# Gates' products by Strassen's algorithm beside the attention, the branches' projections behind it

## The chip, the cores and the metric

The kernel runs on one core of one Trainium2 chip. The metric is the device time of one execution, in microseconds (us), median of three runs; the kernel before takes 1975.72 us (1972.22 to 1982.68). A core has a matrix engine (TensorE, PE in the profile, which also shows its weight loads as PEld), a vector engine (VectorE, DVE), an engine for activations and copies (ScalarE, ACT), a general engine (GpSimd, POOL), and queues from which DMAs are issued; this kernel issues nearly all of them from SyncE (SP). SBUF is the memory on the chip, PSUM the banks that matmuls accumulate into.

## The reference

One layer over 1024 tokens of width 1024, all in float32. The part that the change touches:

```python
z_a, z_bx, z_by, z_q, z_k, z_v, z_g = split_cols(h @ w_in[l], IN_SIZES)      # h = rms_norm(x)
y_a = rwkv7_mixer(z_a, ...) @ proj_a[l]                     # 512 x 1024
y_b = rglru_mixer(z_bx, z_by, ...) @ proj_b[l]              # 512 x 1024
y_c = dilated_attention_mixer(z_q, z_k, z_v, ...) @ proj_c[l]   # 256 x 1024
gates = jax.nn.sigmoid(z_g.reshape(bsz, seq, N_BRANCHES, D_MODEL))
merged = gates[:, :, 0] * y_a + gates[:, :, 1] * y_b + gates[:, :, 2] * y_c
x = x + merged @ w_out[l]
...
x = x + jnp.square(jax.nn.relu(u)) @ mlp_down[l]            # u = rms_norm(x) @ mlp_up[l]
```

`z_g` has 3 x 1024 columns. The attention has three groups of four heads, with dilations 1, 4 and 16; their outputs are weighted by their softmax denominators and summed to the 256 rows of y_c.

## The kernel before, in words

Activations lie transposed, channels on the 128 partitions and tokens along a row. A matmul takes 128 channels x 128 columns of weights against 128 x 512 tokens (a half), into one PSUM bank. To hold float32 accuracy each operand is split in a high part and a low part (`hi` is a cast by ScalarE, `lo` the difference, by GpSimd or VectorE), and `mm3` issues three matmuls for one product: high by high (L233), high by low (L234), low by high (L235). `load_w` reads weights into `wraw`, a ring of two buffers, and splits them into `whi` and `wlo`, rings of three.

The stages follow each other: norm and RG-LRU, then RWKV with the projections of Q, K and V between its steps, then from 799.4 to 1259.9 us the attention with the gates and the branches' projections, then `w_out` and the MLP.

In that third stage the attention runs in six units, two chunks `cc` of 128 channels times three groups `g`. A unit loads its Q and K (`load`: two tiles `z0`, `z1`), scales K and loads the bias (`prep`), and then goes through four steps `sp`: logits `l` on TensorE (L1014), the bias and the maximum on VectorE (`lg`, `nm`), the exponential on ScalarE (L1033), transposes `pt` (L1044), a copy by ScalarE, and the products with V, `o` (L1059). `combine_rows` transposes a unit's maxima and sums (`stt`, L1068) and sends them through DRAM (`st_d`, then `row`). `combine(cc)` makes the weights of the groups of one chunk, sends them through DRAM (`cw_d`), spreads them over the partitions (`cb`), and sums the groups' outputs to a half of `yc`.

Between these steps `filler` hands out pieces of the generator `fill`, so that TensorE has wide products while the other engines work. They come from `gate_ab` (the products `zg` and projections `pj` of the branches b and a) and `gate_c_z` (`zg` of branch c); `gates_c` does branch c's projection behind the attention. A `zg` piece is a half of a column tile, 24 matmuls, followed by a tanh; a `pj` piece has 12 matmuls for a half, and VectorE multiplies it with (1 + tanh). The partial sums of the branches go through DRAM as `mg_d`. The split branches, `yh` and `yl`, are made from `yb_d`, `ya_d` and `yc_d`, the raw rows (`yr`) passing through `wraw`.

Each engine works through its instructions in order. A scheduler with a simulated timeline sets that order when the kernel is built; within it, `tc.issue_after(pins[-lag].ins)` keeps a filler from being issued before the logits of a tile some steps back. SP hands out its DMAs in order too: one that must wait holds those behind it.

Of the kernel before, what the change touches and what calls it, by code (L numbers as in the profile page):

```python
# [18 lines left out]
P = 128  # L19
# [105 lines left out]
def hybrid_block(ctx, tc, io, out, dbg=None):  # L125
# [15 lines left out]
    yc_d = dr.tile([P, T], F32, name="yc_d")  # L141
# [99 lines left out]
    def gemm_pieces(w2d, c0, n, hh, hl, nm, evac, w=None, halves=(0, 1)):  # L241

        hi, lo = w or load_cols(w2d, c0, n, nm)
        for hf in halves:
            ps = pg.tile([P, 512], F32, tag="g", name=f"g_{nm}_{hf}")
            mm3(ps[:n, :], [(hi[:, k, :], lo[:, k, :], hh[hf][:, k, :], hl[hf][:, k, :]) for k in range(KT)])
            evac(ps, hf)
            yield
# [10 lines left out]
    def norm_split(xns, gkey, hh, hl, ks, nm):  # L259

        for k in ks:
            ps = psum("w", 2, f"nt_{nm}{k}")
            for i in range(4):
                PE.transpose(ps[:, i * P : (i + 1) * P], xns[i][:, k * P : (k + 1) * P], ident)
            gcol = pc(gkey, k)
            last = A.activation(hh[:, k, :], ps, AF.Copy, scale=gcol)
            V.scalar_tensor_tensor(hl[:, k, :], ps, gcol, hh[:, k, :], ALU.mult, ALU.subtract)
        return last

    w_in = io["w_in"][0]  # L270
# [55 lines left out]
    ths, yc, pws = {}, [], []  # L326

    def load_pc(m):

        raw = wp.tile([P, 2, 256], F32, tag="wraw", name=f"p2r{m}", bufs=2)  # L330
        S.dma_start(raw, io["proj_c"][0][:, m * P : (m + 2) * P].rearrange("(k p) c -> p k c", p=P))
        wh = gt.tile([P, 2, 256], F32R, tag="pwh", name=f"p2h{m}", bufs=1)
        wl = gt.tile([P, 2, 256], F32R, tag="pwl", name=f"p2l{m}", bufs=1)
        A.copy(wh, raw)
        G.tensor_tensor(wl, raw, wh, ALU.subtract)
        return wh, wl

    gt_p = tc.tile_pool(name="gt", bufs=1)
    gt = gt_p.__enter__()
    gy = gt  # L340
    gy_p = tc.tile_pool(name="gy", bufs=1)
    gy2 = gy_p.__enter__()
    zs = gate_c_z(tc, pieces, gt, ths)

    def fills():
        yield from gate_ab(tc, io, pieces, pg, gt, gy2, wp, ya_d, yb_d, load_w, mm3)
        for cc in range(2):
            yc.append([gt.tile([P, T], F32R, tag=t, name=f"{t}2{cc}", bufs=2) for t in ("yh", "yl")])
        raw = wp.tile([P, T], F32, tag="wraw", name="yr2", bufs=2)
        S.dma_start(raw, yc_d)  # L350
        A.copy(yc[0][0], raw)
        V.tensor_tensor(yc[0][1], raw, yc[0][0], ALU.subtract)
        pws.append(load_pc(0))
        for _ in range(4):
            next(zs)
            yield

    fill = fills() if "mixers_only" not in dbg else iter(())
    if "no_attn" not in dbg:
        attention(tc, io, dbg, psum, der, cg, yc_d, yc, bias_d, sst, rk_d, cw_d, v_d, qk_d, fill)  # L360
    for _ in fill:
        pass
    gy_p.__exit__(None, None, None)
    if "mixers_only" in dbg:
        gt_p.__exit__(None, None, None)
        hpool.__exit__(None, None, None)
        return
# [14 lines left out]
def attn_values(tc, io, hh, hl, load_w, mm3, pg, wp, v_d):  # L382
# [4 lines left out]
    for g in range(3):  # L387
        wv = [load_w(w_in[512 * q : 512 * q + 512, C_VV + 256 * g : C_VV + 256 * g + 256].rearrange("(k p) c -> p k c", p=P),
                     [P, 4, 256], f"wv{g}{q}") for q in range(2)]
        for s in range(8):  # L390
            ts_ = slice(s * P, (s + 1) * P)
            ps = pg.tile([P, 512], F32, tag="g", name=f"v{g}{s}")
            mm3(ps[:, 0:256], [(hh[:, k, ts_], hl[:, k, ts_], wv[k // 4][0][:, k % 4, :], wv[k // 4][1][:, k % 4, :]) for k in range(KT)])
# [578 lines left out]
def attention(tc, io, dbg, psum, der, cg, yc_d, yc, bias_d, sst, rk_d, cw_d, v_d, qk_d, fill):  # L972
# [4 lines left out]
    with tc.tile_pool(name="ac", bufs=1) as ac, tc.tile_pool(name="au", bufs=2) as au:  # L977
        zt, rqks, vts, biases, stats, ogs, pins = {}, {}, {}, {}, {}, {}, []

        def load(cc, g):  # L980
            for x in range(2):
                z = zt[(cc, g, x)] = au.tile([P, T], F32, tag=f"z{x}", name=f"z{x}_{g}{cc}", bufs=2)
                S.dma_start(z, qk_d[g, x, cc])

        def prep(cc, g):

            u = f"{g}{cc}"
            bias = biases[(cc, g)] = au.tile([P, 2, 256], F32, tag="bias", name=f"bias{u}", bufs=2)
# [90 lines left out]
        def combine(cc):  # L1079
# [24 lines left out]
            for hf in range(2):  # L1104
# [12 lines left out]
                if cc == 0:  # L1117
                    S.dma_start(yc_d[:, sl], y)
                elif yc:
                    A.copy(yc[1][0][:, sl], y)  # L1120
                    V.tensor_tensor(yc[1][1][:, sl], y, yc[1][0][:, sl], ALU.subtract)
# [17 lines left out]
        load(*units[1])  # L1139
        for n, (cc, g) in enumerate(units):  # L1140
# [23 lines left out]
        filler(7, 1)  # L1164
# [25 lines left out]
def gate_ab(tc, io, pieces, pg, gt, gy2, wp, ya_d, yb_d, load_w, mm3):  # L1190
# [3 lines left out]
    steps = [(b, m) for b in (1, 0) for m in range(KT)]  # L1194
    ys, wts, ths = {}, {}, {}

    def z_steps(b, m):

        def ev(ps, hf):
            th = ths[(b, m, hf)] = gt.tile([P, H], F32, tag="th", name=f"th{b}{m}{hf}", bufs=4)  # L1200
            A.activation(th, ps, AF.Tanh, scale=0.5)

        yield from pieces(C_Z + b * D + m * P, P, f"zg{b}{m}", ev)

    def load_y(b):
        for k in range(4):
            raw = wp.tile([P, T], F32, tag="wraw", name=f"yr{b}{k}", bufs=2)
            S.dma_start(raw, (yb_d if b else ya_d)[k * P : (k + 1) * P, :])
            pool = gt if k < 2 else gy2
            h = pool.tile([P, T], F32R, tag="yh", name=f"yh{b}{k}", bufs=2)  # L1210
            l = pool.tile([P, T], F32R, tag="yl", name=f"yl{b}{k}", bufs=2)
            A.copy(h, raw)
            (G if k % 2 else V).tensor_tensor(l, raw, h, ALU.subtract)
            ys[(b, k)] = (h, l)

    def proj_steps(b, m):
        if m % 2 == 0:
            w = io["proj_b" if b else "proj_a"][0][:, m * P : (m + 2) * P]
            wts[b] = load_w(w.rearrange("(k p) c -> p k c", p=P), [P, 4, 256], f"p{b}{m}")
        if m == 0:  # L1220
            load_y(b)
        wh, wl = wts[b]
        ms = slice((m % 2) * P, (m % 2 + 1) * P)
        for hf in range(2):
            sl = slice(hf * H, hf * H + H)
            th = ths.pop((b, m, hf))
            if b == 0:
                tb = gt.tile([P, H], F32, tag="tb", name=f"tb{m}{hf}", bufs=2)
                S.dma_start(tb, io["mg_d"][0][m, :, sl])
            ps = pg.tile([P, 512], F32, tag="g", name=f"pj{b}{m}{hf}")  # L1230
            mm3(ps, [(wh[:, k, ms], wl[:, k, ms], ys[(b, k)][0][:, sl], ys[(b, k)][1][:, sl]) for k in range(4)])
            V.scalar_tensor_tensor(th, th, 1.0, ps, ALU.add, ALU.mult)  # L1232
            if b == 0:
                G.tensor_tensor(th, th, tb, ALU.add)
            S.dma_start(io["mg_d"][1 - b][m, :, sl], th)
            yield

    yield from z_steps(*steps[0])
    for i, s in enumerate(steps):
        if i + 1 < len(steps):  # L1240
            yield from z_steps(*steps[i + 1])
        yield from proj_steps(*s)


def gate_c_z(tc, pieces, gt, ths):

    for m in range(KT):

        def ev(ps, hf):
            th = ths[(m, hf)] = gt.tile([P, H], F32, tag="th", name=f"th2{m}{hf}", bufs=4)  # L1250
            tc.nc.scalar.activation(th, ps, AF.Tanh, scale=0.5)

        yield from pieces(C_Z + 2 * D + m * P, P, f"zg2{m}", ev)


def gates_c(tc, io, psum, gt, zs, ths, mhi, mlo, yc, load_pc, pw, mm3):
# [3 lines left out]
    for m in range(KT):  # L1260
        if m % 2 == 0:
# [392 lines left out]
```

## Time and profile before

| | us |
|---|---|
| median of three runs | 1975.72 (1972.22 to 1982.68) |
| profiled execution | 1980.51 |
| its span | 1978.7 |
| norm and RG-LRU, RWKV | 0 to 799 |
| attention, gates, projections | 799.4 to 1259.9 |
| w_out | 1259.9 to 1354 |
| MLP up, MLP down | 1354 to 1650, 1650 to 1979 |

The profile is of one execution. A line of a group gives the line of the kernel, the engine, the operation, the tile written and the tiles read, shape and count, then the busy time in us and the mean of one in ns, then the idle time ahead of it and what ended that. A row by stage gives the stretch, its length, and for PE, PEld, DVE, ACT and POOL the busy time with the number of instructions, then the granted clock of TensorE, the DMA share and GB/s. A row of the waits gives who waited for whom, the total in us, how often, and the longest. A row of the timeline gives start, duration, engine, line and operation, with the idle time ahead in brackets. An SP row's duration is that of handing out; when the data is there is seen from who waits for it.

### The profile page before, as it was taken

The numbers are of one execution on the slowest core, as the hardware profiler recorded it, in microseconds if no ns is written. First come the engines' busy times: TensorE is split into PE (matmuls) and PEld (weight loads), VectorE is DVE, ScalarE is ACT, GpSimd is POOL, SyncE is SP. The second block draws the span as 40 slices with busy tenths as digits, with TensorE's granted clock in tenths as the row PEclk, the third lists the DMA queues.
The fourth block names the chain that finished last, engine by engine and source line by source line (L and its number), as shares of the span: only waits on it lengthen the run. The fifth ranks groups of instructions, "written<-read, shape, count | busy, mean of one in ns | idle before, by whom it ended". The sixth has DMA issues, their size and how long they took to land. (4 is left out here: it accounts for less than half of the span.)

```text
span 1978.7 us, 29639 instructions
## 1 busy us (share of the span) xinstructions
PE 1918.6 (97%) x11754; PEld 1528.5 (77%) x11754; DVE 1143.5 (58%) x1868; ACT 717.3 (36%) x1184; POOL 727.8 (37%) x590
## 2 busy tenths in 40 slices
PE   8999999999999999899999999999999999999999
PEld 6776677787677878777777778887888888888887
DVE  5546356657656564323333344436877567988875
ACT  5675223243333331333334322245323323333332
POOL 1333434442452340211263242244343343444543
PEclk9999999999999998999999999999999999999999
DMA  4122312222221221633354333552433439544231
GB/s 147 54 61 79 91 52 62 55 60 52 54 70 40 66 65 38 197 121 102 100 170 128 102 116 99 185 183 107 158 140 149 163 136 381 195 146 181 96 123 69
DMA packets 187056, 227.08 MB, mean 115 GB/s; under 512 B 38072, under 2 KB 132949, under 8 KB 186918
## 3 DMA queue, kind: packets, MB, share of 16 engines
q1 hardware_dynamic: 186742, 225.18, 34.7%
q8 instruction: 92, 1.51, 0.3%
q14 instruction: 46, 0.38, 0.1%
q0 software_dynamic: 160, 0.02, 0.0%
q10 hardware_dynamic: 16, 0.00, 0.0%
HBM read 163.42 MB, written 64.10 MB: 115 GB/s over the span
## 5 line engine op out<-in xcount | busy, mean ns | idle before, releaser
L233 PE MATMUL g_zg<-hh,wh_zg 128*128 128x512 f32 x384 | 155.3, 404 | 0.0
L234 PE MATMUL g_zg<-hl,wh_zg 128*128 128x512 f32 x384 | 152.5, 397 | 0.0
L235 PE MATMUL g_zg<-hh,wl_zg 128*128 128x512 f32 x384 | 152.3, 397 | 0.0
L1374 POOL TENSOR_TENSOR wl_d<-dr,wh_d 128x1024 fp32r<-128x1024 f32 x40 | 101.0, 2525 | 127.5 <-ACT wh_d L1373 116.2
L1374 DVE TENSOR_TENSOR du<-dq,du 128x1024 fp32r<-128x1024 f32 x56 | 124.0, 2215 | 23.5 <-ACT du L1373 22.8
L226 POOL TENSOR_TENSOR wl_zg<-wr_zg,wh_zg 128x1024 fp32r<-128x1024 f32 x24 | 57.5, 2395 | 164.1 <-ACT wh_zg L225 143.2
L233 PE MATMUL dx<-wh_d,du 128*128 128x512 f32 x256 | 99.7, 389 | 0.5 <-DVE acc L1554 0.5
L234 PE MATMUL dx<-wl_d,du 128*128 128x512 f32 x256 | 99.6, 389 | 0.0
L235 PE MATMUL dx<-wh_d,du 128*128 128x512 f32 x256 | 99.5, 389 | 0.0
L1373 ACT CAST wh_d<-dr 128x1024 fp32r<-128x1024 f32 x40 | 42.1, 1052 | 142.1 <-PE dx L235 72.8
L233 PEld LDWEIGHTS g_zg<-hh,wh_zg 128*128 128x128 f32 x384 | 73.0, 190 | 18.0 <-issue 3.6
L235 PEld LDWEIGHTS g_zg<-hh,wl_zg 128*128 128x128 f32 x384 | 72.8, 190 | 16.5 <-issue 1.5
L234 PEld LDWEIGHTS g_zg<-hl,wh_zg 128*128 128x128 f32 x384 | 72.9, 190 | 15.7 <-issue 1.8
L234 PE MATMUL g_z<-hl,wh_z 128*128 128x512 f32 x192 | 77.1, 402 | 0.0
L235 PE MATMUL g_z<-hh,wl_z 128*128 128x512 f32 x192 | 77.0, 401 | 0.0
L233 PE MATMUL g_z<-hh,wh_z 128*128 128x512 f32 x192 | 76.5, 399 | 0.4 <-DVE zsq L428 0.4
L773 DVE TENSOR_SCALAR s<-ac,wc 64x64 f32<-64x64 f32 x128 | 36.0, 281 | 69.2 <-PE ac L769 66.8
L1374 POOL TENSOR_TENSOR wl_a<-ur,wh_a 128x1024 fp32r<-128x1024 f32 x15 | 46.8, 3117 | 72.9 <-ACT wh_a L1373 72.9
L1374 POOL TENSOR_TENSOR wl_s<-ur,wh_s 128x1024 fp32r<-128x1024 f32 x16 | 42.5, 2658 | 79.2 <-ACT wh_s L1373 79.2
L1232 DVE SCALAR_TENSOR_TENSOR th<-th,pj 128x512 f32<-128x512 f32 x32 | 21.8, 684 | 73.7 <-PE pj L235 71.3
L226 POOL TENSOR_TENSOR wl_wo<-wr_wo,wh_wo 128x1024 fp32r<-128x1024 f32 x16 | 38.4, 2403 | 68.4 <-ACT wh_wo L225 68.4
L1033 ACT ACTIVATE lg<-lg,nm 128x128 f32<-128x128 f32 (+1 forms) x96 | 42.2, 441 | 56.6 <-DVE nm L1031 56.6
(664 smaller groups left out, 5706.4 us busy)
## 6 DMA issues: line engine op xcount, KB each, us to landing
dq<-u_d SPq DMA_DIRECT2D x56, 512.0 KB
ur<-in_mlp_up_dram SPq DMA_DIRECT2D x16, 1024.0 KB
dr<-in_mlp_down_dram SPq DMA_DIRECT2D x16, 1024.0 KB
wr_zg<-in_w_in_dram SPq DMA_DIRECT2D x24, 512.0 KB
mg_d<-th SPq DMA_DIRECT2D x32, 256.0 KB
tb<-mg_d SPq DMA_DIRECT2D x32, 256.0 KB
wr_wo<-in_w_out_dram SPq DMA_DIRECT2D x16, 512.0 KB
wr_z<-in_w_in_dram SPq DMA_DIRECT2D x12, 512.0 KB
```

The source lines that it names most:

```text
L226: E.tensor_tensor(lo, raw, hi, ALU.subtract)
L233: PE.matmul(ps, lh, rh, start=first and i == 0, stop=False, skip_group_check=skip)
L234: PE.matmul(ps, lh, rl, start=False, stop=False, skip_group_check=skip)
L235: end = PE.matmul(ps, ll, rh, start=False, stop=last and i == n - 1, skip_group_check=skip)
L773: V.tensor_scalar(ns[half[h], :], pb[h][half[h], 128 * j + 64 * c : 128 * j + 64 * c + 64], wc[half[h], 2 * i + c : 2 * i + c + 1], None, ...
L1033: A.activation(lg[:, q, los[q] : 256], lg[:, q, los[q] : 256], AF.Exp, bias=nm[:, q : q + 1], accum_out=stat[:, 1, h, 2 * sp + q : 2 * sp ...
L1232: V.scalar_tensor_tensor(th, th, 1.0, ps, ALU.add, ALU.mult)
L1373: A.copy(hi, src)
L1374: split.last = E.tensor_tensor(lo, src, hi, ALU.subtract)
```

## The change

The products of the gates change from `gate_ab`/`gate_c_z` to `gate_z`. It takes column tiles in twelve pairs. The first two pairs are done as before (`n_plain`). For the other ten, the 2x2 blocks are two column tiles by two halves of k (weights) and two halves of k by two halves of the tokens (activations), and Winograd's form of Strassen's algorithm makes four blocks of result from seven block products. The activations' combinations T1 to T4 are made once, T1, T2 and T4 by VectorE, T3 by GpSimd, with high and low parts; the weights' combinations are made for each pair, three adds and a low part by VectorE, the other low parts by GpSimd. Three of the products are copied from PSUM by ScalarE (`held`) and added by VectorE.

All tanh results go to DRAM (`th_d`) and come back in the new stage `gates`, behind the attention, where all three branches' projections are made and summed. The branch rows y_b are loaded to a pool `yp` opened behind the attention's pools, y_c and y_a through `wraw`. `combine` writes both chunks to `yc_d`.

In the attention, the buffers of Q and K and of the bias are one and not two; the next unit is loaded and prepared after a unit's last step, with three fillers behind. The fillers' counts change to the smaller pieces (12 matmuls each), and the filler(7) ahead of `combine(1)` goes.

```diff
-    hpool = tc.tile_pool(name="hT", bufs=1)
+    hpool = tc.tile_pool(name="hT", bufs=1, side="right")
...
+    fill = gate_z(tc, w_in, ht, h2, hp, gt, wp, pg, th_d, load_cols, mm3, late)
+    attention(tc, io, dbg, psum, der, cg, yc_d, bias_d, sst, rk_d, cw_d, v_d, qk_d, fill)
+    yp_p = tc.tile_pool(name="yp", bufs=1)
+    yp = yp_p.__enter__()
+    ys = {}
+
+    def load_y(pool, src, b, n, raw):
+
+        for k in range(n):
+            r = raw(k)
+            S.dma_start(r, src[k * P : (k + 1) * P, :])
+            h, l = (pool.tile([P, T], F32R, tag=f"y{b}{k}{x}", name=f"y{x}{b}{k}") for x in "hl")
+            A.copy(h, r)
+            (G if k % 2 else V).tensor_tensor(l, r, h, ALU.subtract)
+            ys[(b, k)] = h, l
+
+    yraw = lambda b: lambda k: wp.tile([P, T], F32, tag="wraw", name=f"yr{b}{k}", bufs=2)
+    load_y(yp, yb_d, 1, 4, lambda k: yp.tile([P, T], F32, tag=f"y2{k // 2}{'hl'[k % 2]}", name=f"yr1{k}"))
+    late.append(lambda: load_y(yp, yc_d, 2, 2, yraw(2)))
     for _ in fill:
         pass
...
+    load_y(ya, ya_d, 0, 4, yraw(0))
+    last = gates(tc, io, psum, pg, gt, ya, wp, th_d, ys, mhi, mlo, load_w, mm3)
...
-                z = zt[(cc, g, x)] = au.tile([P, T], F32, tag=f"z{x}", name=f"z{x}_{g}{cc}", bufs=2)
+                z = zt[(cc, g, x)] = au.tile([P, T], F32, tag=f"z{x}", name=f"z{x}_{g}{cc}", bufs=1)
...
-                    filler(1.2)
+                    filler(0.4 if i else 2)
                 V.tensor_copy(ogs[(cc, g)][:, sp * 256 : (sp + 1) * 256], po[:, 0:256])
-                if sp == 0 and n > 0 and n + 1 < 6:
+                if sp == 3 and n + 1 < 6:
                     load(*units[n + 1])
-                if sp == 1 and n + 1 < 6:
                     prep(*units[n + 1])
+                    filler(3)
                 if sp == 2 and n == 3:
                     combine(0)
             combine_rows(cc, g)
-        filler(7, 1)
         combine(1)
...
+        for c in two:
+            total(V, F["T1"][:, c], c, [b("B12", 0, c), b("B11", 0, c), (b("B12", 1, c), add), (b("B11", 1, c), sub)])
+            total(V, F["T2"][:, c], c, [b("B22", 0, c), F["T1"][:, c], (b("B22", 1, c), add)])
+            split(V, "T2", c, F["T2"][:, c])
+            split(V, "T1", c, F["T1"][:, c])
...
+        for j, (nm, bk, first) in enumerate((("B11", X, True), ("B21", Y, True), ("T2", X, False), ("T1", Y, True),
+                                            ("T3", X, False), ("B22", Y, False), ("T4", X, False))):
...
+            wh, wl = ops.pop((n, j))
+            mm3(bk, [(wh[:, k, :], wl[:, k, :], B[nm][0][:, k, :], B[nm][1][:, k, :]) for k in range(4)], first=first, skip=True)
+            if j in (0, 2, 3):
+                t = tile(f"{n}{j}")
+                A.copy(t, bk)
+                held[j] = t
+            elif j < 6:
+                t = held[{1: 0, 4: 3, 5: 2}[j]]
+                V.tensor_tensor(t, bk, t, ALU.add)
+                done(b, *{1: (m0, 0), 4: (m1, 1), 5: (m0, 1)}[j], t, t)
+            else:
+                done(b, m1, 0, tile(f"{n}{j}"), bk)
```

In `gates`, for each of four pairs of column tiles and for the branches b, c, a: `load_w` of the pair's projection (`wr_p`, split to `wh_p`, `wl_p`), four banks `pj`, the four tanh halves reloaded (`tb` for b, `tg` else), the products, then `(1 + tanh) * pj` and the sum over branches on VectorE.

How the order on the engines changes is seen at three places. On TensorE, behind the last unit's `stt21`, the rows of before continue with the last projections of branch a and then with the products of branch c (`g_zg20`, first of sixteen halves):

```order
L1068 MATMUL stt21_10687<-cg_92,stat21_10083 32x128
L233 MATMUL pj070_10718<-yh00_9509,wh_p06_10664 128x512
L234 MATMUL pj070_10718<-yl00_9510,wh_p06_10664 128x512
L235 MATMUL pj070_10718<-yh00_9509,wl_p06_10665 128x512
...
L233 MATMUL g_zg20_0_10772<-hh_85,wh_zg20_10768 128x512
L234 MATMUL g_zg20_0_10772<-hl_86,wh_zg20_10768 128x512
```

Now there are the last products of pair 10 (`zg100`, `zg101`: its two banks), seven block products of pair 11, and then the first four banks of the projection of branch b, which read `wh_p10` and the split rows `yh10`, `yl10`:

```order
L1055 MATMUL stt21_10665<-cg_97,stat21_10248 32x128
L234 MATMUL zg101_10533<-zT1h_7924,wz103_10455 128x512
...
L234 MATMUL zg111_10820<-hh00_84,wz110_10584 128x512
...
L234 MATMUL zg111_10820<-zT4h_8481,wz116_10835 128x512
...
L234 MATMUL pj100_10985<-yh10_10743,wh_p10_10981 128x512
L235 MATMUL pj100_10985<-yl10_10744,wh_p10_10981 128x512
```

Between `stt21` and the first `pj` row there are 132 wide matmuls; before, there were some 500 of them left.

On SP, before, the loads of the rows y_b and y_a and of the first projection weights stand ahead of the attention and in it; the last chunk's end has only these transfers (`cw_d` and `cb`: the groups' weights on their way out and back, `tb`, `mg_d`: partial sums, `wr_zg`: weights of gates, `p2r`: weights of branch c's projection):

```order
L222 DMA wr_zg23_11062<-in_w_in_dram 128x8x128
L331 DMA p2r2_11135<-in_proj_c_dram 128x2x256
L1103 DMA cw_d_76<-row001_9832 16x128
L1103 DMA cw_d_76<-cw11_10892 16x128
L1235 DMA mg1_d_81<-th071_10646 128x512
L1103 DMA cw_d_76<-cw21_10895 16x128
L121 DMA cb100_10911<-cw_d_76 64x512 x2
```

Now the end of that chunk is followed by the loads of all the rows and weights of the projections:

```order
L1104 DMA yc_d_71<-yc11_10718 128x512
L1346 DMA tb100_10989<-th_d_80 128x512
L1346 DMA tb101_11004<-th_d_80 128x512
...
L338 DMA yr10_10741<-yb_d_70 128x1024
L338 DMA yr11_10747<-yb_d_70 128x1024
...
L338 DMA yr00_10955<-ya_d_69 128x1024
...
L338 DMA yr03_10973<-ya_d_69 128x1024
L223 DMA wr_p10_10979<-in_proj_b_dram 128x4x256
```

`yr10` stands behind the write of the last half of y_c, and `wr_p10`, on which the first projection depends, behind eight loads of rows and the reloads of thirteen tanh halves.

On VectorE, where the attention begins, there were two splits of y_b (`yl`) and the scaling of K (`z1`) for the first two units ahead of the first logits:

```order
L1213 TENSOR_TENSOR yl10_8068<-yr10_8065,yh10_8067 128x1024
L997 SCALAR_TENSOR_TENSOR z1_00_7894<-z1_00_7894,der_101,rb000_8018 128x512
L997 SCALAR_TENSOR_TENSOR z1_00_7894<-z1_00_7894,der_101,rb001_8022 128x512
L1213 TENSOR_TENSOR yl12_8080<-yr12_8077,yh12_8079 128x1024
L997 SCALAR_TENSOR_TENSOR z1_10_8029<-z1_10_8029,der_101,rb100_8248 128x512
L997 SCALAR_TENSOR_TENSOR z1_10_8029<-z1_10_8029,der_101,rb101_8252 128x512
L1024 SCALAR_TENSOR_TENSOR lg0000_8041<-l0000_8035,sst_102,bias00_8016 128x128
```

Now T1 and T2 (`fT1`, `fT2`) and T1's low part stand there, with the scaling for the first unit alone:

```order
L1197 TENSOR_TENSOR fT1_7920<-hh01_86,hh00_84 128x1024 x2
L1199 TENSOR_TENSOR fT1_7920<-fT1_7920,hl01_87 128x1024 x2
L1199 TENSOR_TENSOR fT1_7920<-fT1_7920,hl00_85 128x1024 x2
L1197 TENSOR_TENSOR fT2_7921<-hh11_90,fT1_7920 128x1024
L984 SCALAR_TENSOR_TENSOR z1_00_7899<-z1_00_7899,der_106,rb000_7980 128x512
L1206 TENSOR_TENSOR zT1l_7925<-fT1_7920,zT1h_7924 128x1024
...
L984 SCALAR_TENSOR_TENSOR z1_00_7899<-z1_00_7899,der_106,rb001_7984 128x512
L1199 TENSOR_TENSOR fT2_7921<-fT2_7921,hl11_91 128x1024
...
L1011 SCALAR_TENSOR_TENSOR lg0000_7999<-l0000_7993,sst_107,bias00_7978 128x128
```

So the first logits have twelve passes of 128x1024 ahead of them where two stood.

More of the change, by code (lines that the diff above doesn't have):

```diff
@@ L338, in hybrid_block @@
     gt_p = tc.tile_pool(name="gt", bufs=1)
     gt = gt_p.__enter__()
[L340 to L356, printed above, removed]
@@ L358, in hybrid_block @@
-    fill = fills() if "mixers_only" not in dbg else iter(())
-    if "no_attn" not in dbg:
-        attention(tc, io, dbg, psum, der, cg, yc_d, yc, bias_d, sst, rk_d, cw_d, v_d, qk_d, fill)
+    h2_p = tc.tile_pool(name="hS", bufs=1, side="right")
+    h2 = h2_p.__enter__()
+    late = []
+    fill = gate_z(tc, w_in, ht, h2, hp, gt, wp, pg, th_d, load_cols, mm3, late)
+    attention(tc, io, dbg, psum, der, cg, yc_d, bias_d, sst, rk_d, cw_d, v_d, qk_d, fill)
+    yp_p = tc.tile_pool(name="yp", bufs=1)
@@ L969, in lru, with attention @@
     return first
-def attention(tc, io, dbg, psum, der, cg, yc_d, yc, bias_d, sst, rk_d, cw_d, v_d, qk_d, fill):
+def attention(tc, io, dbg, psum, der, cg, yc_d, bias_d, sst, rk_d, cw_d, v_d, qk_d, fill):
     nc = tc.nc
@@ L1187, in bias_tiles, with gate_z @@
             S.dma_start(bias_d[g], bass.AP(tensor=src.tensor, offset=src.offset, ap=[[EW, 4], [0, P], [1, EW]]))
-def gate_ab(tc, io, pieces, pg, gt, gy2, wp, ya_d, yb_d, load_w, mm3):
+def gate_z(tc, w_in, ht, h2, hp, gt, wp, pg, th_d, load_cols, mm3, late):
     nc = tc.nc
     V, A, G, S = nc.vector, nc.scalar, nc.gpsimd, nc.sync
[L1194 to L1205, printed above, removed]
-        for k in range(4):
[L1207 to L1235, printed above, removed]
-            yield
[L1238 to L1242, printed above, removed]
@@ L1245, in gate_c_z @@
[L1245 to L1256, printed above, removed]
+    f32 = lambda ap: ap.bitcast(F32)
+    B = {nm: (ht[(0, kh, hf)], ht[(1, kh, hf)]) for nm, kh, hf in (("B11", 0, 0), ("B12", 0, 1), ("B21", 1, 0), ("B22", 1, 1))}
@@ new lines, in done, with raw @@
+    def done(b, m, hf, th, src):
+        A.activation(th, src, AF.Tanh, scale=0.5)
+        S.dma_start(th_d[b, m, :, hf * H : hf * H + H], th)
+    cols = lambda b, m: w_in[:, C_Z + b * D + m * P : C_Z + b * D + (m + 1) * P].rearrange("(k p) c -> p k c", p=P)
+    count = [0]
+    ops, raws = {}, {}
+    def raw(n):
+        b, p = pairs[n]
+        raws[n] = []
+        for i in range(2):
+            r = wp.tile([P, KT, P], F32, tag="wraw", name=f"wr_z{n}{i}", bufs=2)
+            S.dma_start(r, cols(b, 2 * p + i))
+            raws[n].append(r)
@@ new lines, in gate_z @@
+    plain = [0]
+    comb = combinations()
+    for n in range(n_plain):
+        b, p = pairs[n]
+        for i in range(2):
+            m = 2 * p + i
+            hi, lo = load_cols(w_in, C_Z + b * D + m * P, P, f"zg{b}{m}")
+            if n == n_plain - 1 and i == 1:
+                raw(n_plain)
+            for hf in range(2):
+                ps = pg.tile([P, 512], F32, tag="g", name=f"zg{b}{m}{hf}")
+                for kh in range(2):
+                    mm3(ps, [(hi[:, 4 * kh + k, :], lo[:, 4 * kh + k, :], ht[(0, kh, hf)][:, k, :], ht[(1, kh, hf)][:, k, :]) for k in range(4)],
+                        first=kh == 0, last=kh == 1)
+                    next(comb, None)
+                    if n == n_plain - 1 and i == 1:
+                        operand(n_plain, 2 * hf + kh)
+                    if kh == 1:
+                        done(b, m, hf, t := tile(f"{b}{m}{hf}"), ps)
+                    yield
@@ new lines, in gate_z @@
+    plain.clear()
+    operand(n_plain, 4)
+    operand(n_plain, 5)
+    for n in range(n_plain, len(pairs)):
+        b, p = pairs[n]
+        banks = [pg.tile([P, 512], F32, tag="g", name=f"zg{n}{i}") for i in range(2)]
+        X, Y = banks if n % 2 == n_plain % 2 else banks[::-1]
+        m0, m1 = 2 * p, 2 * p + 1
+        held = {}
+        for j, (nm, bk, first) in enumerate((("B11", X, True), ("B21", Y, True), ("T2", X, False), ("T1", Y, True),
+                                            ("T3", X, False), ("B22", Y, False), ("T4", X, False))):
+            if n == n_plain:
+                next(comb, None)
+            wh, wl = ops.pop((n, j))
[10 more added lines that the diff above has]
+                done(b, m1, 0, tile(f"{n}{j}"), bk)
+            if j == 0:
+                operand(n, 6)
+                if n + 1 < len(pairs):
+                    raw(n + 1)
+            elif n + 1 < len(pairs):
+                operand(n + 1, j - 1)
+            elif j == 1:
+                late[0]()
+            yield
```

164 lines of the change are left out of this document (106 added, 58 removed).

## Prediction

> **What bounds the kernel now.** I read the page's busy times first, then the busy times by stage, then TensorE's waits in the stage that the change rewrites.
>
> ```profile
> PE 1918.6 (97%) x11754; PEld 1528.5 (77%) x11754; DVE 1143.5 (58%) x1868; ACT 717.3 (36%) x1184; POOL 727.8 (37%) x590
> ```
>
> ```profile
> 799.40:1259.90 460.50, 450.00 (x2240) 348.79 (x2239) 171.43 (x354) 147.70 (x374) 140.12 (x83) 0.99 0.41 126
> ```
>
> ```profile
> PE pt L1044 <- ACT lg L1033: 4.1, 1, 4.1
> PE pj L234 <- DVE yl L1121: 2.6, 1, 2.6
> PE pj L234 <- POOL yl L1213: 1.7, 1, 1.7
> PE l L1014 <- DVE lg L1024: 1.2, 1, 1.2
> PE pj L233 <- ACT th L1201: 0.6, 1, 0.6
> ```
>
> TensorE (PE) is busy 97% of the span. Between 799.4 and 1259.9 us, where the attention runs among the gates' products and the branches' projections, it is busy 450.0 of 460.5 us, at a clock of 0.99, and all its waits add up to 10.2 us. VectorE, ScalarE and GpSimd are busy 171, 148 and 140 us there. So this stage takes as long as its matmuls plus what TensorE waits, and two questions decide: how many matmuls go, and what TensorE is left to do while something else is late.
>
> **What goes.** A pair of column tiles of the gates takes 96 matmuls before (two tiles, two halves, 8 blocks of k, 3 products of high and low parts), 7 x 12 = 84 by the seven products. Ten pairs of twelve change: 12 x 96 = 1152 (three rows of 384 like the first below) becomes 2 x 96 + 10 x 84 = 1032, and 120 go.
>
> ```profile
> L233 PE MATMUL g_zg<-hh,wh_zg 128*128 128x512 f32 x384 | 155.3, 404 | 0.0
> ```
>
> ```profile
> 818.20 0.39 PE L233 MATMUL g_zg<-hh,wh_zg 128*128 128x512 f32 x1
> 818.42 0.39 PE L234 MATMUL g_zg<-hl,wh_zg 128*128 128x512 f32 x1
> 818.65 0.39 PE L235 MATMUL g_zg<-hh,wl_zg 128*128 128x512 f32 x1
> 818.88 0.39 PE L233 MATMUL g_zg<-hh,wh_zg 128*128 128x512 f32 x1
> ```
>
> The 404 ns of one are pipelined; what counts is start to start, 0.68 us for three, 0.2267 each. 120 x 0.2267 = **27.2 us** less. The 480 matmuls of the projections only move. The waits of `pj` on `yl` and on `th` (2.6 + 1.7 + 0.6 = **4.9 us**) go with the old order of the steps; what is late instead is the next part.
>
> **The junction behind the attention.** Before, the split y_b and y_a were loaded during the attention, and TensorE still had some 115 us of products when the last unit's `stt` (L1068) had run at 1143.9. Now all projections stand behind the attention. The order on TensorE shows 132 matmuls of 128x512 between `stt21` and the first `pj100`: 132 x 0.2267 = 29.9 us, with three small ones 30.2 (the part on the change shows the rows). On SP's queue the loads of y_b (`yr10` to `yr13`) stand behind the last write of y_c, whose buffer they overlay; the loads of y_a and the first weights (`wr_p10`) stand behind those. So the projections can't begin before this chain is through, and I time it by the same steps of before.
>
> ```profile
> 1143.89 0.28 PE L1068 MATMUL stt<-cg,stat 128*32 128x128 f32 x1
> ```
>
> ```profile
> 1144.71 0.33 SPq L1071 DMA_DIRECT2D st_d<-st  x1
> 1146.76 1.33 SPq L1076 DMA_DIRECT2D row<-st_d  x4
> ```
>
> ```profile
> 1179.59 1.29 POOL L1116 TENSOR_TENSOR yc<-yc,yt 128x512 f32<-128x512 f32 x1 [1.91 <-DVE yt L1115]
> ```
>
> From `stt` to the end of the last sum of y_c (the rows' round trip, the weights, their spreading as `cb`, the products and sums) took 1180.88 - 1143.89 = 37.0 us. After the change the casts of y_c and the projections' passes no longer stand between, so I take 35 (33 to 37). The write of y_c must land: from `st_d` to the read that waits for it is 1146.76 - 1144.71 = 2.05 us. Then come the loads.
>
> ```profile
> 799.93 0.32 SPq L1208 DMA_DIRECT2D yr<-yb_d  x1
> ...
> 803.78 1.05 ACT L1212 CAST yh<-yr 128x1024 fp32r<-128x1024 f32 x1 [4.56 <-DMA yr<-yb_d]
> ...
> L1213 DVE TENSOR_TENSOR yl<-yr,yh 128x1024 fp32r<-128x1024 f32 x4 | 5.1, 1271 | 10.2 <-ACT yh L1212 10.2
> ...
> L1213 POOL TENSOR_TENSOR yl<-yr,yh 128x1024 fp32r<-128x1024 f32 x4 | 9.5, 2379 | 20.8 <-ACT yh L1212 20.8
> ```
>
> One load of 512 KB and its cast: 3.85 us from issue to the cast's start, 1.05 the cast, 1.27 the difference on VectorE (2.38 on GpSimd). The raw buffers are a ring of two, so the loads follow one another through VectorE's differences. Counted from `stt21`: y_c landed 37; `yr10` cast and split, then `yl12` and `yl20` on VectorE, 3.85 + 1.05 + 3 x 1.27 = 8.7, and 1.4 more as `yr12` is the third of four loads: 47. `yr00` takes the buffer of `yr20`: 3.85 + 1.05 + 1.27 = 6.2, 53.3. `yr02` the buffer of `yr00`: 59.5. `wr_p10` the buffer of `yr02`: 3.85 + 1.05 = 4.9, 64.4. Ahead of `yr00` on SP stand 13 reloads of tanh halves of 256 KB, 3.4 MB.
>
> ```profile
> GB/s 147 54 61 79 91 52 62 55 60 52 54 70 40 66 65 38 197 121 102 100 170 128 102 116 99 185 183 107 158 140 149 163 136 381 195 146 181 96 123 69
> ```
>
> The most that any slice moved is 381 GB/s, so 3.4 MB takes at least 9 us; a third of it I count in the chain's way, 3 us: **67 us**. TensorE has 30 us of work, so it waits **37 us**. The bounds: were every load as quick as the 2.05 us of the small write, the chain is 33 + 2.05 + (2.05 + 1.05 + 3.8) + 2 x 4.37 + 3.1 = 54, a wait of 24. For the upper end I take the Q and K load below, 7.7 us: 37 + 2 + (7.7 + 1.05 + 3.8) + 2 x 10.0 + 8.75 = 80, a wait of 50. I take 37 because 3.85 was measured on the same load. The low part of the weights (GpSimd, 2.4 us) comes behind `yl03`, and the first eight matmuls (1.8 us) don't need it: +1.
>
> A wait of this length also costs after its end.
>
> ```profile
> 835.47 1.18 PE L1044 MATMUL pt<-cg,lg 128*128 128x128 f32 x3 [4.09 <-ACT lg L1033]
> 836.30 0.77 PE L233 MATMUL g_zg<-hh,wh_zg 128*128 128x512 f32 x1
> ...
> 840.50 0.52 PE L235 MATMUL g_zg<-hh,wl_zg 128*128 128x512 f32 x1
> 840.86 0.40 PE L233 MATMUL g_zg<-hh,wh_zg 128*128 128x512 f32 x1
> ```
>
> After the idle 4.09 us the products stand 0.42 us apart until 840.9 and 0.23 after it: some nine of them at about half rate, **2 us**.
>
> **The attention.** Its fillers are now 1032 matmuls of products, less the 132. Three things differ. First, the combinations of the activations stand on VectorE ahead of the first logits: 12 passes of 128x1024, 1.27 each, 15 us, where two splits and the next unit's Q and K stood. TensorE has 115 wide matmuls (26 us) ahead of its first transposes. I leave the wait of 4.1 us there as it is, 0 to 6 more. Second, with one buffer for Q and K the next unit loads when the unit before has ended.
>
> ```profile
> 966.28 0.92 SPq L983 DMA_DIRECT2D z<-qk_d  x2
> ```
>
> ```profile
> 974.00 1.42 DVE L997 SCALAR_TENSOR_TENSOR z<-z,der,rb 128x512 f32<-128x512 f32 x2 [3.17 <-DMA z<-qk_d]
> ```
>
> That load took 7.7 us, and the scaling 1.4, so 9.1. The order has 36 wide matmuls there, 8.2 us, and the last tile's transposes: 0 to 2 us for each of five boundaries, and I take 0.6. Third, the first combine shares its buffers and SP with the next unit's load: 0 to 5 us, I take 1. Together **+4** (0 to 15). GpSimd and ScalarE have more, shorter work: per pair six low parts of 128x512 and seven casts in place of two passes of 128x1024 each; ScalarE's 148 us and GpSimd's 140 of 460 leave room. The projections behind come next.
>
> ```profile
> L1232 DVE SCALAR_TENSOR_TENSOR th<-th,pj 128x512 f32<-128x512 f32 x32 | 21.8, 684 | 73.7 <-PE pj L235 71.3
> L1272 DVE TENSOR_TENSOR th<-th,tb 128x512 f32<-128x512 f32 x13 | 18.6, 1432 | 0.5
> L1274 DVE SCALAR_TENSOR_TENSOR ml<-th,mh 128x512 fp32r<-128x512 f32 x12 | 11.0, 916 | 9.1 <-ACT mh L1273 9.1
> ```
>
> The 480 projections behind take 108.8 us, 27.2 for two column tiles; for these VectorE has 12 x 0.68 + 8 x 1.43 + 4 x 0.92 = 23.3 us, so TensorE bounds there.
>
> **The sum**, on the profiled execution of 1980.5 us: -27.2 - 4.9 + 37 + 1 + 2 + 4 = **+12**, 1992.4 us. The median 1975.7 is 0.24% below that execution, so 1992.4 x 0.9976 = **1988 us**.
>
> **The rivals.** (1) The wait at the junction is near its lower bound, 24 us, since the loads are quicker than at 800 us. Then -32.1 + 24 + 1 + 2 + 4 = -1, about 1975 us. It speaks for it that little else loads then; against it that this little is 3.4 MB of reloads.
>
> ```profile
> 1162.66 0.69 DVE L1111 TENSOR_TENSOR yc<-cb,og 128x512 f32<-128x512 f32 x1 [5.03 <-DMA cb<-cw_d]
> ```
>
> ```profile
> 1163.38 8.04 SPq L121 DMA_DIRECT2D cb<-cw_d  x6
> ```
>
> (2) The other side, faster: the combine behind `stt21` is much shorter without the projections beside it. SP spent 8.0 us on handing out six of the `cb`, and VectorE waited 5.0 us for the first; with these 13 us gone the combine takes 24 us and not 37, and y_c lands 11 us sooner than I count. With the loads at their lower bound too the chain is 54 - 9 = 45 us, a wait of 15, and that is the point from which it decides: -32.1 + 15 + 1 + 2 + 4 = -10. With a wait of 10 it is 1961 us. Against it: the `cb` go through the same queue and the same small buffers as before, and each row of a load. (3) The attention becomes bound by its latencies: thin fillers between its steps, one buffer, and slower passes on VectorE while GpSimd works.
>
> ```profile
> L1374 DVE TENSOR_TENSOR du<-dq,du 128x1024 fp32r<-128x1024 f32 x56 | 124.0, 2215 | 23.5 <-ACT du L1373 22.8
> ```
>
> The same pass on VectorE took 2.2 us in the last stage, where GpSimd has its passes beside it, against 1.27 alone. With this factor the 15 us ahead of the first logits are 26, TensorE waits some 6 us more, and the boundaries 2 us each: +16 in place of +4, about 2000 us. The Trainium skill ("GPSIMD Engine Reference", § 1. Specifications) says that the two share their SBUF interfaces where a VectorE instruction has two operands in SBUF; the row agrees, and by that rule the sum is +24, by the 1.27 us of the attention's own passes +12. (4) That the change doesn't do what it says: the order has 1032 products, so I give it nothing.
>
> **Chances.** The forecast 0.56 (its own range 1981 to 1997: a wait of 30 to 46), rival 1 0.18, rival 2 0.10, rival 3 0.16. A measurement of this kernel tells 0.5%, 9.9 us, from no change: below 1965.8 is faster, above 1985.6 slower. Faster: rival 2 and a little of rival 1, 0.12. Same: the rest of rival 1, and of the forecast the part with waits of under 35, 0.30. Slower: 0.58. The range leaves out most of rival 2 and the tail of rival 3: 1966 to 2004.
>
> **What would show it.** TensorE's waits in the profile of the changed kernel should hold one `pj` wait of 24 to 50 us, released by ScalarE's cast of the first projection weights, with a chain back through SP to the write of y_c; the products' starts at 0.227 us; a slow stretch of 2 us behind the wait; `pt` and `l` waits of under 15 us in all. I am wrong if that one wait is missing or under 15, if VectorE's `lg` releases most of the idle time, or if the products come slower than 0.23 us apart.

## The result, and the profile after

The changed kernel takes 2005.78 us in the median (1999.78 to 2010.26, four runs), against 1977.82 (four runs) for the kernel before: a ratio of 1.014, 95% interval 1.0101 to 1.018. It is slower, as forecast, but by 28 us and not by 12, and the time lies 2 us above the end of the range. The two profiled executions, on which the rest of this section rests, are 24 us apart (spans of 1978.7 and 2002.7).

TensorE's waits in the changed kernel over the whole program, of which these rows belong to the rewritten stage (who waited for whom, total, times, longest):

```profile
PE pj L234 <- ACT wh_p L226: 37.2, 1, 37.2
...
PE l L1001 <- DVE lg L1011: 0.8, 2, 0.6
...
PE pt L1031 <- ACT lg L1020: 0.7, 1, 0.7
PE zg L234 <- DVE th L1310: 0.7, 1, 0.7
```

One wait, for the first projection weights, is 37.2 us; all the others of the attention are under 1 us each. By stretches (start and end, length, then PE, PEld, DVE, ACT and POOL, the clock, the DMA share and GB/s), the wait and the projections behind it:

```profile
1136.70:1173.90 37.20, 0.02 (x2) 0.04 (x1) 9.08 (x7) 12.51 (x13) 13.87 (x7) 0.56 0.71 254
1173.90:1285.00 111.10, 111.10 (x480) 91.79 (x481) 74.10 (x92) 20.82 (x27) 30.90 (x14) 0.98 0.44 145
```

TensorE stands still, and VectorE, ScalarE and GpSimd are idle for most of that stretch too; the DMA engines are busy for 0.71 of it. The timeline of SP, ScalarE and TensorE shows the chain that it waits for; the last unit's `stt` starts at 1104.0:

```profile
1138.36 0.33 SPq L1104 DMA_DIRECT2D yc_d<-yc  x1
...
1140.82 1.93 SPq L338 DMA_DIRECT2D yr<-yb_d  x4
...
1155.77 10.61 SPq L338 DMA_DIRECT2D yr<-ya_d  x4
1169.39 0.38 SPq L223 DMA_DIRECT2D wr_p<-in_proj_b_dram  x1
```

```profile
1146.77 2.09 ACT L340 CAST yh<-yr 128x1024 fp32r<-128x1024 f32 x2 [8.09 <-DMA yr<-yb_d]
...
1172.75 1.04 ACT L226 CAST wh_p<-wr_p 128x1024 fp32r<-128x1024 f32 x1 [2.25 <-DMA wr_p<-in_proj_b_dram]
```

```profile
1173.89 0.76 PE L234 MATMUL pj<-yh,wh_p 128*128 128x512 f32 x1 [37.18 <-ACT wh_p L226]
1174.46 0.63 PE L235 MATMUL pj<-yl,wh_p 128*128 128x512 f32 x1
1174.88 0.63 PE L234 MATMUL pj<-yh,wh_p 128*128 128x512 f32 x1
```

The last half of y_c is sent 34 us behind `stt`, y_b is asked for at 37, y_a at 52, the weights at 65, and the first projection runs at 70. The projections that follow are 0.42 us apart at first.

So the large term came out as forecast, and the missing time lies elsewhere. In the next table all starts of matmuls are summed to the start of the next, by what they make (worked out from the matmul records of the two profiled executions). The stage runs from the last `g` of RWKV to the first `wo`.

| us | forecast | before | after | difference |
|---|---|---|---|---|
| products of the gates, without the wait | -27.2 | 277.8 | 257.4 | -20.4 |
| the wait | +37 | | 37.2 | +37.2 |
| projections, with their waits and slow start | -4.9 + 1 + 2 | 117.2 | 111.1 | -6.1 |
| the attention's small matmuls l, pt, o, stt | +4 | 65.7 | 75.2 | +9.5 |
| the stage | +12 | 460.7 | 481.0 | +20.3 |
| what lies ahead of it | 0 | 799.4 | 804.0 | +4.6 |
| w_out and MLP | 0 | 718.6 | 717.7 | -0.9 |

Four rows are off: the products saved 7 us less, the small matmuls cost 5.5 us more than the 4 us of the attention, the norm, RG-LRU and RWKV stages, whose algorithm isn't changed, took 4.6 us more, and the projections came out 4 us better. A run of the timeline in the changed kernel, in the first two pairs of the gates' products, which are done in the classical way, shows a cause that the first and the third of these can share:

```profile
809.84 0.40 PE L236 MATMUL zg<-hh,wl_zg 128*128 128x512 f32 x1
810.07 0.40 PE L234 MATMUL zg<-hh,wh_zg 128*128 128x512 f32 x1
810.30 0.40 PE L235 MATMUL zg<-hl,wh_zg 128*128 128x512 f32 x1
810.53 0.40 PE L236 MATMUL zg<-hh,wl_zg 128*128 128x512 f32 x1
810.77 0.40 PE L234 MATMUL zg<-hh,wh_zg 128*128 128x512 f32 x1
811.00 0.40 PE L235 MATMUL zg<-hl,wh_zg 128*128 128x512 f32 x1
```

Five steps take 1.16 us, 0.232 each; before, the same instruction started every 0.2267. The granted clock from 800 to 830 us is 1.00 in both profiles, and the projections of the changed kernel are 0.2267 apart. What these slow products have in common is the operand that streams by: the activations' tiles `hh` and `hl`, which the change moves to the other side of SBUF. By their addresses in the built program they start at 163808 and on, 32 bytes past a multiple of 64; before, at 52224, a multiple of 1024. `yh`, `mh`, and the MLP's operands, which are at multiples of 1024 in both kernels, are read at 0.2267.

### The profile page after: what moved, and what is told of

The parts are those of the page before. It is cut to its first block, busy times and chain, and to the rows that moved or that the text cites. A ratio compares the mean times of both kernels' runs of the same rounds, so it can differ in the third digit from the quotient of the medians.

```text
span 2002.7 us, 29779 instructions
## 1 busy us (share of the span) xinstructions
PE 1915.3 (96%) x11634; PEld 1513.3 (76%) x11634; DVE 1248.2 (62%) x1992; ACT 762.9 (38%) x1275; POOL 769.1 (38%) x631
## 5 line engine op out<-in xcount | busy, mean ns | idle before, releaser
L1267 POOL TENSOR_TENSOR wz<-wr_z,wz 128x512 fp32r<-128x512 f32 x60 | 80.2, 1339 | 164.3 <-ACT wz L1266 139.3
L234 PE MATMUL pj<-yh,wh_p 128*128 128x512 f32 x160 | 63.6, 397 | 37.2 <-ACT wh_p L226 37.2
L1455 POOL TENSOR_TENSOR wl_a<-ur,wh_a 128x1024 fp32r<-128x1024 f32 x15 | 47.6, 3175 | 75.2 <-ACT wh_a L1454 75.2
L234 PEld LDWEIGHTS pj<-yh,wh_p 128*128 128x128 f32 x160 | 30.7, 192 | 44.1 <-POOL yl L341 37.6
L235 PE MATMUL pj<-yl,wh_p 128*128 128x512 f32 x160 | 63.4, 396 | 0.0
L236 PE MATMUL pj<-yh,wl_p 128*128 128x512 f32 x160 | 62.0, 390 | 0.0
L1454 ACT CAST du<-dq 128x1024 fp32r<-128x1024 f32 x56 | 58.6, 1046 | 2.0 <-DMA dq<-u_d 2.0
L1635 DVE TENSOR_TENSOR acc<-dx,acc 128x512 f32<-128x512 f32 x64 | 42.0, 680 | 26.3 <-PE dx L236 26.3
L234 PE MATMUL v<-wh_wv,hh 128*128 128x256 f32 x192 | 55.9, 291 | 0.6 <-DVE st L766 0.6
```

Of the source, the lines that this page charges most:

```text
L234: PE.matmul(ps, lh, rh, start=first and i == 0, stop=False, skip_group_check=skip)
L235: PE.matmul(ps, lh, rl, start=False, stop=False, skip_group_check=skip)
L236: end = PE.matmul(ps, ll, rh, start=False, stop=last and i == n - 1, skip_group_check=skip)
L1267: (V if i == 2 else G).tensor_tensor(l, src, h, ALU.subtract)
L1454: A.copy(hi, src)
L1455: split.last = E.tensor_tensor(lo, src, hi, ALU.subtract)
```

## The experiments

All runs are compared with the kernel before on their own chip, 1977 to 1979 us in each set.

**Where the activations lie.** Unused bytes at the end of the activations' pool shift its tiles and the combinations T1 to T4.

```diff
+    hp.tile([P, 8], F32, name="padh")
     hx = lambda x, hf, k: ht[(x, k // 4, hf)][:, k % 4, :]
```

> The changed kernel with 32 unused bytes behind the activations' pool, which shifts its tiles (and T1 to T4) from 32 bytes past a multiple of 64 to a multiple of 64. Theory P (placement): a 512-wide matmul that reads a tile 32 bytes off costs 0.233 us and not 0.227; here the gates' products, and the RWKV stage's, go back to 0.227 to 0.229, the RWKV stage ends at 799 to 800 us and not 804, and the time falls by 9 to 11 us to 1995 to 1997. Rival Q (the side, the eight separate tiles or the sharing with other engines makes them slow): the products stay at 0.233 and the time within 2 us of 2006. The wait at the junction stays at 37 us in both.

It took 2004.56 us (ratio 1.0137, 1.0112 to 1.0162). The products stayed at 0.233 us: at an odd multiple of 64 bytes nothing is gained. In its profile the third stage still began at 800.3 us and not at 804.0, with the same step; so a single profile's figure for the work ahead doesn't tell the cause. The opposite experiment, in the kernel before:

```diff
+    hp.tile([P, 8], F32, name="padh0")
     hh_t = hp.tile([P, KT, T], F32R, name="hh")
     hl_t = hp.tile([P, KT, T], F32R, name="hl")
+    hp.tile([P, 56], F32, name="padh1")
```

> The kernel before with 32 unused bytes ahead of its activations' buffers, so that they start 32 bytes past a multiple of 64; 224 more bytes behind them. P: all products that read them cost 0.233 us, RWKV ends at 804, the whole takes 9 to 12 us more, 1986 to 1990. Q: no change, 1976 to 1979.

It took 1991.56 us, ratio 1.0073 (1.005 to 1.0097), so some 13 us more with the program otherwise as before (the pools behind lie 256 bytes further). The steps account for it: 1680 matmuls ahead of the stage at 0.0041 us more and 1152 products at 0.0054 more (0.2278 to 0.2332 in the mean) are 13 us. Its timeline in the gates' products:

```profile
821.77 0.40 PE L235 MATMUL g_zg<-hh,wh_zg 128*128 128x512 f32 x1
822.00 0.39 PE L236 MATMUL g_zg<-hl,wh_zg 128*128 128x512 f32 x1
822.24 0.40 PE L237 MATMUL g_zg<-hh,wl_zg 128*128 128x512 f32 x1
822.47 0.39 PE L235 MATMUL g_zg<-hh,wh_zg 128*128 128x512 f32 x1
822.70 0.40 PE L236 MATMUL g_zg<-hl,wh_zg 128*128 128x512 f32 x1
822.94 0.39 PE L237 MATMUL g_zg<-hh,wl_zg 128*128 128x512 f32 x1
```

Steps of 0.233, where the same kernel had 0.2267. So it is the place, and neither the side of SBUF nor the eight tiles. How fine the place must be, three more runs tell, with 480, 96 and 224 bytes (120, 24 and 56 elements) in the first edit:

> The changed kernel with 480 unused bytes behind the activations' pool: its tiles and T1 to T4 at multiples of 512 bytes, where the run with 32 had them at an odd multiple of 64 and stayed at 0.233 us. P2 (a finer placement than 64 bytes decides): the products go to 0.227 to 0.229 us, the time to 1994 to 1998. Q: 0.233 stays, 2003 to 2006.

> The changed kernel with 96 unused bytes: the activations' tiles at an odd multiple of 128 bytes. If 128 bytes is the placement that counts, products at 0.227 to 0.229 us; if only 256 or 512 will do, 0.233 as at 64.

> The same with 224 bytes: an odd multiple of 256. 0.227 to 0.229 us where 128 or 256 counts, 0.233 where only 512 does.

| run | the tiles' start | step of the Q and K products | time |
|---|---|---|---|
| changed kernel | 32 past a multiple of 64 | 0.2330 | 2005.78 |
| 32 bytes | odd multiple of 64 | 0.2332 | 2004.56 |
| 96 bytes | odd multiple of 128 | 0.2324 | 2002.47, one run |
| 224 bytes | odd multiple of 256 | 0.2290 | 1996.93, one run |
| 480 bytes | multiple of 512 | 0.2291 | 1997.59 |
| before, 32 bytes off | 32 past a multiple of 64 | 0.2331 | 1991.56 |
| before | multiple of 1024 | 0.2290 | 1977.82 |

The step is the mean, over the some 480 pairs of neighbours in `g_z` (the products of Q and K) that are under 0.26 us apart. In the run with 224 bytes a stretch reads

```profile
809.85 0.39 PE L237 MATMUL zg<-hh,wl_zg 128*128 128x512 f32 x1
810.08 0.39 PE L235 MATMUL zg<-hh,wh_zg 128*128 128x512 f32 x1
810.31 0.39 PE L236 MATMUL zg<-hl,wh_zg 128*128 128x512 f32 x1
810.53 0.39 PE L237 MATMUL zg<-hh,wl_zg 128*128 128x512 f32 x1
810.76 0.39 PE L235 MATMUL zg<-hh,wh_zg 128*128 128x512 f32 x1
810.99 0.39 PE L236 MATMUL zg<-hl,wh_zg 128*128 128x512 f32 x1
```

The border lies between 128 and 256 bytes. The 480 bytes made the changed kernel 8 us faster (ratio 1.0101, 1.007 to 1.0132, where it was 1.014; the two intervals overlap, so the size is less sure than the step). Between the profiles it is 3.1 us in the stage and 2.4 in the work ahead; by the steps it should be 1680 x 0.004 + 1032 x 0.0042 = 11 us. Why 128 bytes don't do, no run shows.

**What stands behind the last unit.** Fewer fillers in the attention leave more products for the end.

```diff
-                    filler(0.4 if i else 2)
+                    filler(0.3 if i else 1.4)
```

> The changed kernel with fewer fillers in the attention (1.4 and 0.3 pieces for a tile's two steps in place of 2 and 0.4), so about 250 matmuls stand behind the last unit and not 132. Theory J (the 37 us are what the chain of y_c, rows and weights is longer than the work behind the last unit, and the attention has room): the wait falls to 10 to 16 us, the attention ends some 27 us sooner, the time is 1980 to 1985. Rival L (the attention would be bound by its own latencies with fewer fillers): its waits on lg, z and ptS grow by what the junction saves, 2000 to 2008.

It took 1993.95 us (1.0083, 1.0061 to 1.0105). The waits of the stage:

```profile
PE pj L234 <- ACT wh_p L226: 14.5, 1, 14.5
PE zg L234 <- DVE th L1310: 5.6, 3, 3.2
PE pt L1031 <- ACT lg L1020: 2.1, 2, 1.4
PE l L1001 <- DVE lg L1011: 1.8, 3, 1.0
```

The wait fell by 22.7 us, as J has it, but the time only by 12, to a place between the ranges of J and L. The products waited 5 us more for VectorE's sums of the products before (`th`), the logits took 2.8 us more, and a product in the attention, with its changes to other work, 0.2542 us in place of 0.2503. So the attention has room, but not for all of it: J with a part of L.

> Both edits of the two runs before, that of the 32 bytes in the changed kernel and that of the fillers. P and J together: 1970 to 1976. P alone: 1995 to 1997. J alone: 1980 to 1985. If the two share a cause: less than the sum.

1993.83 us (1.0081, 1.0053 to 1.0109), as the fillers alone: the 32 bytes add nothing here either.

**The order of the loads.** `load_y(ya, ya_d, ...)` is called in `gates`, behind the `load_w` of branch c's first weights, and no longer ahead of `gates`.

```diff
-    load_y(ya, ya_d, 0, 4, yraw(0))
...
             wh, wl = load_w(w.rearrange("(k p) c -> p k c", p=P), [P, kn, 256], f"p{b}{p}")
+            if p == 0 and b == 2:
+                more()
```

> The changed kernel with the loads of y_a moved from ahead of the first projection weights to behind the second ones. J (the chain through the ring of two raw buffers sets the first projection): wr_p10 is issued where yr00 was, 13.6 us sooner, the wait is 22 to 25 us, a new one of 0 to 5 us comes before the projection of y_a: 1992 to 1997. Rival M (the rate of memory sets it, 0.7 of the DMA engines' time in that stretch): the weights come under 5 us sooner, 2000 to 2005.

1995.3 us (1.0093, 1.0069 to 1.0118). The wait is 26.2 us, a little over J's 22 to 25, and no other of note came in its place:

```profile
PE pj L234 <- ACT wh_p L226: 26.4, 2, 26.2
PE pj L236 <- POOL wl_p L227: 0.8, 1, 0.8
```

SP hands out the load of the weights here:

```profile
1155.50 0.38 SPq L223 DMA_DIRECT2D wr_p<-in_proj_b_dram  x1
```

The last unit's `stt` starts at 1103.6 here, so the weights are asked for 52 us behind it and not 65, and the wait is 11 us shorter. That is J's chain, of loads that follow each other through the ring of two raw buffers, and more than M allows, which has the weights under 5 us sooner. But the load of the weights itself took longer, 5.8 us from issue to cast (1161.33) where it had taken 3.4, so the transfers beside it count too; how much of the chain is theirs no run separates.

**The products themselves.** All twelve pairs in the classical way in the changed kernel; T1 to T4 and the weights' combinations are gone.

```diff
-    n_plain = 2
+    n_plain = 12
...
-            if n == n_plain - 1 and i == 1:
-                raw(n_plain)
+            if n == n_plain - 1 and i == 0:
+                late[0]()
...
```

The second part puts the load of the rows of y_c, which stood at the second product of the last pair, ahead of the products of the last two column tiles.

> The changed kernel with all twelve pairs done in the classical way (n_plain 12, no combinations), 1152 products, 215 of them behind the last unit. Theory W (the saved products only lengthened the wait at the junction, since the chain behind the last unit is what ends last there): +28 us of products, but the wait falls from 37 to about 19, and the logits l, which TensorE now gets in alternating heads again, cost about 27 us and not 33: 2005 to 2012. Rival S (each saved product is time saved): +27 to 2032.

2005.94 us (1.0143, 1.0117 to 1.017): 120 matmuls more, and the same time as the changed kernel. The waits:

```profile
PE zg L234 <- ACT wh_zg L226: 16.6, 1, 16.6
PE pj L234 <- ACT wh_p L226: 2.8, 1, 2.8
PE pt L1031 <- ACT lg L1020: 1.0, 1, 1.0
```

The wait is 19.4 us in place of 37.2, now mostly at the last tile's weights, which follow the rows of y_c through the ring of raw buffers. Without the waits the products took 286.9 us, 29.5 more than in the changed kernel. So of these 29.5 us that the seven products save, 17.8 go into a longer wait, 5.6 into the logits (32.6 us and not 27.0), some 4 into the other small matmuls and 1.5 into the projections. In TensorE's order the logits of a tile's two heads stand side by side 57 times and of one head 4 times; in the changed kernel it is 30 and 20, before 66 and 3. That neighbours of different heads are what makes them cheap is argued from these counts only.

**All together**: 480 bytes, the fillers of 1.4 and 0.3, and the later load of y_a.

> The changed kernel with the 480 bytes, the thinner fillers (1.4 and 0.3) and the later load of y_a together; 242 products behind the last unit. P2 and J: -10 for the placement, -11 for the fillers, -11 more for the load, so 1968 to 1978, at or under the kernel before. If P2 fails: 1980 to 1988.

1975.47 us over ten runs, before 1978.01: a ratio of 0.9983, 0.9968 to 0.9998. It is as fast as the kernel before, or faster by less than half a per cent. The gain of 30.3 us on the changed kernel is the sum of the three gains alone (8.2 + 11.8 + 10.5). What still waits:

```profile
PE zg L235 <- DVE th L1310: 8.0, 6, 2.9
PE pj L235 <- ACT wh_p L227: 5.6, 1, 5.6
PE l L1001 <- DVE lg L1011: 2.8, 3, 1.1
PE pt L1031 <- ACT lg L1020: 2.2, 2, 1.4
```

With fillers between those of the changed kernel and these, 1.7 and 0.3:

> The run with all three edits, but fillers of 1.7 and 0.3: 206 products behind the last unit and not 242, and the logits' heads alternate more often in TensorE's order (38 neighbours of different heads, 14 of the same; 23 and 28 with 1.4). If the thin fillers cost the 8.6 us that l takes over before, l falls by 3 to 5 us and the wait at the junction grows by about as much: 1972 to 1978, no difference that can be told. If the waits for the products' own sums (8 us) come from the thin fillers, 1966 to 1970.

1987.08 us (1.0041, 1.0022 to 1.006), outside both expectations: products waited 11.8 us for `th`, the projections 8.4, the logits 4.6 for `lg`. The logits' row is 35.6 us, but 3.5 of it is a wait of a product that stands behind a logit; without waits it is 32.1, and 33.8 in the run of 1.4, so it fell by 1.7 us where 3 to 5 were expected. In the profiles the stage is 7.2 us longer than with 1.4 (464.5 against 457.3), and the waits account for 6.9 of these; 4.7 more lie ahead of it, in code that is the same. Why this order waits more stays open; the scheduler makes another order for each number.

Last, the same three edits with all pairs classical:

> The run with all three edits (e8), but all twelve pairs in the classical way: 1152 products, 335 or more of them behind the last unit. W (saved products are time saved once no wait absorbs them): +27.5 us for 120 products at 0.229, less what waits and dearer logits the seven products bring with them (8 us on their own sums, 6 at the projections, 6 in l): 1983 to 1998, slower than e8. Rival (the combinations and the denser changes between kinds of work eat the gain): within 4 us of e8's 1975.

1980.62 us (1.0012, 0.9996 to 1.0028), under W's figures and just above the rival's. One wait is left:

```profile
PE zg L235 <- ACT th L1234: 6.8, 1, 6.8
```

By the medians the classical way is slower by 5 us and not by 27, and the two intervals just overlap. With the waits among them the 1152 products took 285.2 us and the 1032 took 263.8: the seven products gave 21.4 us on TensorE and lost 8.1 at the projections (116.9 against 108.8), 3.9 in the logits and 2.9 in `pt` and `o`. That leaves 6.5 of the stage's 6.8 us.

## Why the prediction was right or wrong

- **The wait at the junction**: 37 us forecast, 37.2 measured, released by ScalarE's cast of the first weights as said. Its steps, counted from `stt21`: last sum of y_c 35 forecast, 34.3 measured (1137.07 + 1.27 - 1104.0); y_b asked for 37 and 36.8; y_a 47 and 51.8; the weights 59.5 and 65.4; first projection 67 and 69.9. The chain was 3 us longer than forecast, in the step from asking for y_b to asking for y_a: 15.0 us and not 10, as the first cast of y_b began 5.95 us after the request (1140.82 to 1146.77) and not 3.85. TensorE's own work took 32.7 us, not 30.2. The two misses cancel, so that the figures agree to 0.2 us is luck; that they agree to 3 us is not. The order and the rows of before carried this, and the runs with the later load (26.2 us) and with more work behind the unit (14.5) show the mechanism.
- **The products**: -27.2 forecast, -20.4 measured. The step that failed is the price "0.2267 each" for all of them. It was read from a stretch without the attention and from a kernel whose activations lay well. The gates' products read misplaced tiles, 0.233 us apart, which the prediction itself had named as a sign of being wrong ("slower than 0.23 us apart"). That is 3 of the 7 us: with well placed tiles the products took 254.6 us (480 bytes) and 254.3 (224 bytes), not 257.4. The other 4 are argued from counts: 900 of 1032 products now stand ahead of the last `stt`, among the attention's small matmuls, at 0.250 us each with their changes (0.247 with the 480 bytes); before, it was 768 of 1152, at 0.247, and the rest cost 0.2295. The projections left that mix, which fits their coming out 4 us better than forecast.
- **The attention**: +4 forecast with waits as its substance. The waits were absent (0.7 for `pt`, where I left 4.1 and more; no boundary of a unit shows one), so the single buffer of Q and K and the combinations on VectorE show no wait of their own. In their place the small matmuls took 9.5 us longer, though before's figure holds 4.7 us of waits (4.1 and 0.6); 5.6 of it the run with classical products gives back in the logits. So this term was 5.5 us too small, and its reason was the wrong one.
- **What lies ahead**: the sum put it at nothing, without a reason. The moves of matmuls were weighed, the move of the activations' pool was not. Over the whole program, products included, it costs 11 us by the steps, and by the medians 13 in the kernel before and 8 in the changed one. How much of it lies ahead is less sure: with steps of 0.233 us the third stage began at 800.3 to 806.1 us in seven profiles, 804.0 in the mean, and with 0.229 at 797.1 to 801.8 in six, 800.4 in the mean. With this term 1988 becomes 1996 to 2001; without it the measured time would lie inside the range. The rest up to 2005.78 is in the other rows, and 4 us in the medians' being 28 us apart where the profiles are 24.
- **The rivals**: the short junction (1) and the quick combine (2) fell with the 37.2 us. Rival 3 came nearest to the time, with 2000, but not by its reason: T1's and T2's passes at 1.2 to 1.8 us on VectorE held nobody up.

```profile
L1199 DVE TENSOR_TENSOR fT<-fT,hl 128x1024 f32<-128x1024 f32 x6 | 7.1, 1219 | 0.0
...
L1197 DVE TENSOR_TENSOR fT<-hh,fT 128x1024 f32<-128x1024 f32 x2 | 3.5, 1766 | 0.0
```

- **The saved products against the wait**: the forecast set -27 against +37 without saying that the one feeds the other. The classical run shows it: in the changed kernel the seven products brought nothing (2005.94 against 2005.78), since 18 of the 29.5 us went into the wait and most of the rest into the small matmuls. With the wait shortened they are worth some 5 us (1975.47 against 1980.62).

## What to carry to other kernels

Products saved on an engine that is 97% busy are time saved only if it then has something to do; first find what must be through before the next stage's first instruction, and count the work left for TensorE against it. Where a change moves a pool, look at the addresses of the operands that matmuls stream, in every stage that reads them, also those whose code is the same. A price from start to start should come from the surroundings in which the instruction will stand, not from an undisturbed stretch.

## What the runs showed of the hardware

A matmul that streams 512 float32 columns from SBUF started every 0.229 us (0.2267 undisturbed) where its tiles began at an odd multiple of 256 bytes, at 512 or at 1024, 0.2324 at odd multiples of 128, and 0.233 at odd multiples of 64 and 32 bytes off, at the same granted clock (1.00 from 800 to 830 us in these profiles); the matmuls that hold these tiles as weights didn't become slower (`v`: 0.124 in the changed kernel, 0.126 with the 480 bytes). Behind the idle stretch of 37 us, in which the granted clock was 0.56, the projections were 0.42 us apart for some nine steps, as the products behind the 4 us of before.
